# A decoder layer on one core: token-major x loaded and squared along the second column block, and a final scale folded into one product

## The chip, the core and the metric

The kernel runs on one core of a Trainium2 chip. It is judged by its device time in microseconds (us), the median of three runs: 1476.53 us (1476.25 to 1477.11). Inside the core, TensorE (PE) multiplies matrices into PSUM, VectorE (DVE) and ScalarE (ACT) do elementwise work, GpSimd (POOL) a little of it, and SyncE (SP) issues DMAs. Each engine takes its own list of instructions in order and waits on semaphores. ACT issues DMAs too, from the same list as its arithmetic.

## What is computed

One decoder layer over 256 tokens of width 2048, in float32. Cut to what matters here:

```python
h = rms_norm(x, norm_mix)
q, k, v, cx, cb, cc, ga, gc = split_in_proj(h @ w_in)     # 10240 columns
q = partial_rope(heads(q, 8), pos); k = partial_rope(heads(k, 8), pos)
...                                                       # attention, short convolution, gated merge
x = x + merged @ w_mix_out
...                                                       # cross-attention over 256 memory tokens
u = relu(rms_norm(x, norm_mlp) @ w_up)
x = x + (u * u) @ w_down
return rms_norm(x, norm_final)

def rms_norm(x, g):
    return x * rsqrt(mean(x * x, axis=-1) + 1e-6) * g
```

## The kernel before

Every weight is streamed from HBM once, in pieces of 256 rows by 512 columns (512 KB, `load_w`, issued by SP into six raw buffers). To keep float32 accuracy each piece is split (`split_w`, L61): ACT copies it rounded to the matmul type (`whi`, L66), DVE subtracts that from the raw piece (`wlo`, L67). The activations are split in the same way, and `tok_steps` (L97) makes three matmuls for each 128 rows and each half of the tokens: high times high, high times low, low times high. `tok_group` (L107) runs 16 such steps over a block of 512 columns, into two PSUM banks of the five that the matmuls share. Five pairs of split buffers stand between ACT and DVE on one side and PE on the other.

The norm of x is not applied ahead of the first projection. The feature-major copy of x (`xraw`, loaded from a transposed input) is multiplied by the gain and split (`split_scaled`, L133, into `hT`), and the factor of each token, `r1`, is multiplied in when a result leaves PSUM (`scaled`, L203, on ACT at L204). For `r1` the token-major x (`xtok`, four pieces of 512 KB) is loaded by ACT (L246), ACT squares it in eight pieces with a running sum (`sumsq`, L187, at L189), and `rstd` (L191) makes the factor on DVE and POOL. `xtok` is also the residual stream of everything that follows.

The column blocks at the start come in the order q, k, v (512 columns each), and again q, k, v. The first q block is written out by hand at L236 to L254: for each pair of steps x is scaled, the weights are split and matmuls run; the first four steps are single ones with loads of 128 and 256 KB, the rest pairs. The program gives the four x loads at the end of that block, and the squares behind them. In what order each engine takes its instructions is settled by a scheduler that reads the program and its dependences. A q or k block is rotated on DVE (`rotate`, L213) and transposed on PE (`qk_features`, L224).

At the end, the last 512 columns of the last projection are computed in three cuts: 512 columns for the first half of the tokens, then 256 and 256 for the second half (L494). Behind each cut `add_last` (L462) adds to the residual on DVE (L459), squares on ACT and multiplies by the final gain `gf` (L466); then the norm factor `rf` is made (L508 to L513), four pieces of 512 columns are multiplied by it (L514 to L519), and SP stores them (L520).

## Time and profile before

| | |
|---|---|
| median of three runs | 1476.53 us (1476.25 to 1477.11) |
| the profiled execution | 1476.77 us, span 1475.0 us |
| mean granted TensorE clock | 0.996 |
| PE, DVE, ACT busy | 1454.8, 820.9, 691.2 us |
| DMA | 281.27 MB, mean 191 GB/s |

The span runs from the first to the last instruction; the 1.8 us between it and the execution's time lie around it. A busy time adds up an engine's instructions. A row of a timeline has the start, the duration, the engine with the line of the program, what it writes and reads, and in brackets how long the engine stood idle and what released it. Tiles go by the names of the program's buffers: `S` stands for the large ones (`hT`, `xraw`, later ones), `raw`, `whi` and `wlo` for the weights, `tok` for `xtok`, `acc` for the PSUM banks of the matmuls, `junk` for what the squares write. Matmuls are pipelined and their ends modelled, so the distance from start to start tells their pace.

### The profile page before, as it was taken

The numbers are of one execution on the slowest core, as the hardware profiler recorded it, in microseconds if no ns is written. First come the engines' busy times: TensorE is split into PE (matmuls) and PEld (weight loads), VectorE is DVE, ScalarE is ACT, GpSimd is POOL, SyncE is SP. The second block draws the span as 40 slices with busy tenths as digits, with TensorE's granted clock in tenths as the row PEclk, the third lists the DMA queues.
The fourth block names the chain that finished last, engine by engine and source line by source line (L and its number), as shares of the span: only waits on it lengthen the run. The fifth ranks groups of instructions, "written<-read, shape, count | busy, mean of one in ns | idle before, by whom it ended". The sixth has DMA issues, their size and how long they took to land.

```text
span 1475.0 us, 18233 instructions
## 1 busy us (share of the span) xinstructions
PE 1454.8 (99%) x7064; PEld 1222.4 (83%) x7064; DVE 820.9 (56%) x976; ACT 691.2 (47%) x905; POOL 13.6 (1%) x21
## 2 busy tenths in 40 slices
PE   6999999999999999999999999999999999999997
PEld 5888888888888888888888888888888888888886
DVE  5545555765554646654476655556545555556554
ACT  6444544454444445554564443444434443445442
POOL 0000000000000000000000000000000000000011
PEclk9999999999999999999999999999999999999999
DMA  9666655576666667655555566565565556665652
GB/s 337 193 193 180 184 165 178 170 227 190 187 196 188 186 197 230 212 192 180 172 171 185 187 198 191 182 197 180 194 200 179 193 188 191 192 191 179 198 189 85
DMA packets 145158, 281.27 MB, mean 191 GB/s; under 512 B 8880, under 2 KB 9520, under 8 KB 144944
## 3 DMA queue, kind: packets, MB, share of 16 engines
q1 hardware_dynamic: 141888, 272.66, 58.9%
q10 hardware_dynamic: 3184, 7.45, 1.5%
q8 instruction: 55, 0.90, 0.2%
q14 instruction: 31, 0.25, 0.1%
HBM read 277.98 MB, written 2.10 MB: 190 GB/s over the span
## 4 chain that ended last, share of the span: by engine, by line
PE 98%; DMA 1%; ACT 1%; issue 0%; DVE 0%; POOLq 0%; POOL 0%; DVEq 0%; SPq 0%; ACTq 0%
PE acc L104 23%; PE acc L105 23%; PE acc L103 23%; PE acc L78 15%; PE acc L79 8%; PE aps L145 1%; PE acc L82 1%; DMA tok<-in_x_dram 1%; PE acc L81 1%; DMA raw<-in_w_in_dram 0%; ACT junk L189 0%; PE aps L315 0%; PE aps L270 0%; PE aps L438 0%; PE aps L407 0%
## 5 line engine op out<-in xcount | busy, mean ns | idle before, releaser
L67 DVE TENSOR_TENSOR wlo<-raw,whi 128x1024 fp32r<-128x1024 f32 (+1 forms) x510 | 618.7, 1222 | 561.2 <-ACT whi L66 547.5
L66 ACT ACTIVATE whi<-raw 128x1024 fp32r<-128x1024 f32 (+1 forms) x510 | 532.9, 1055 | 564.1 <-PE acc L105 386.2
L103 PE MATMUL acc<-whi,S 128*128 128x512 f32 x1512 | 584.9, 388 | 11.4 <-ACT whi L66 11.4
L105 PE MATMUL acc<-whi,S 128*128 128x512 f32 x1512 | 587.9, 389 | 0.0
L104 PE MATMUL acc<-wlo,S 128*128 128x512 f32 x1512 | 586.3, 388 | 0.3 <-DVE wlo L67 0.3
L103 PEld LDWEIGHTS acc<-whi,S 128*128 128x128 f32 x1512 | 284.6, 188 | 68.8 <-ACT whi L66 12.7
L78 PE MATMUL acc<-S,whi 128*128 128x512 f32 x960 | 341.6, 398 | 0.0
L104 PEld LDWEIGHTS acc<-wlo,S 128*128 128x128 f32 x1512 | 284.5, 188 | 58.8 <-DVE wlo L67 1.6
L105 PEld LDWEIGHTS acc<-whi,S 128*128 128x128 f32 x1512 | 284.7, 188 | 56.2
L79 PE MATMUL acc<-S,wlo 128*128 128x256 f32 x960 | 269.7, 281 | 0.0
L78 PEld LDWEIGHTS acc<-S,whi 128*128 128x128 f32 x960 | 180.4, 188 | 41.3
L79 PEld LDWEIGHTS acc<-S,wlo 128*128 128x128 f32 x960 | 181.3, 189 | 3.1
L474 ACT ACTIVATE blk<-acc 128x256 f32<-128x256 f32 x64 | 24.3, 380 | 36.0 <-PE acc L82 35.8
L189 ACT ACTIVATE junk<-tok 128x512 f32<-128x512 f32 (+1 forms) x33 | 20.2, 613 | 37.7 <-DVE tok L459 23.6
L459 DVE SCALAR_TENSOR_TENSOR tok<-acc,q,tok 128x512 f32<-128x512 f32 (+1 forms) x33 | 24.1, 731 | 18.0 <-PE acc L105 18.0
L130 ACT ACTIVATE S<-blk 128x512 fp32r<-128x512 f32 x32 | 20.0, 626 | 25.7 <-DVE blk L478 25.7
L475 DVE TENSOR_TENSOR blk<-acc,blk 128x256 f32<-128x256 f32 x64 | 27.0, 422 | 8.0 <-ACT blk L474 8.0
L131 DVE TENSOR_TENSOR S<-blk,S 128x512 fp32r<-128x512 f32 x32 | 22.1, 692 | 9.9 <-ACT S L130 8.4
L82 PE MATMUL acc<-S,whi 128*128 128x512 f32 x64 | 25.6, 400 | 0.0
L478 DVE SCALAR_TENSOR_TENSOR blk<-blk 128x512 f32<-128x512 f32 x32 | 22.0, 689 | 0.6
L204 ACT ACTIVATE blk<-acc,r 128x512 f32<-128x512 f32 x18 | 12.4, 689 | 15.5 <-PE acc L105 15.5
L81 PE MATMUL acc<-S,wlo 128*128 128x256 f32 x64 | 18.1, 283 | 0.0
(127 smaller groups left out, 466.2 us busy)
## 6 DMA issues: line engine op xcount, KB each, us to landing
raw<-in_w_in_dram SPq DMA_DIRECT2D x158, 512.0 KB, 4.2
raw<-in_w_up_dram SPq DMA_DIRECT2D x128, 512.0 KB, 4.0
raw<-in_w_down_dram SPq DMA_DIRECT2D x128, 512.0 KB, 4.3
raw<-in_w_mix_out_dram SPq DMA_DIRECT2D x32, 512.0 KB, 4.9
raw<-in_w_attn_out_dram SPq DMA_DIRECT2D x16, 512.0 KB, 4.3
raw<-in_w_conv_out_dram SPq DMA_DIRECT2D x16, 512.0 KB, 4.5
raw<-in_wkv_x_dram SPq DMA_DIRECT2D x16, 512.0 KB, 4.2
raw<-in_wq_x_dram SPq DMA_DIRECT2D x8, 512.0 KB, 3.9
```

The costliest lines, as they stand in the source:

```text
L66: nc.scalar.activation(hi[:, k:k + step, :], raw[:, k:k + step, :], AF.Copy)
L67: nc.vector.tensor_sub(lo[:, k:k + step, :], raw[:, k:k + step, :], hi[:, k:k + step, :].bitcast(F32))
L78: nc.tensor.matmul(ps, a, xs(k, 2), start=(k == 0), stop=False)
L79: nc.tensor.matmul(ps[:, S:], c, xs(k, 0), start=False, stop=False)
L81: nc.tensor.matmul(ps[:, S:], c, xs(k, 0), start=False, stop=False)
L82: nc.tensor.matmul(ps, a, xs(k, 2), start=(k == 0), stop=True)
L103: nc.tensor.matmul(ps, xh, wh, start=(k == 0), stop=False)
L104: nc.tensor.matmul(ps, xh, wl, start=False, stop=False)
L105: nc.tensor.matmul(ps, xl, wh, start=False, stop=(k == nk - 1))
L459: nc.vector.scalar_tensor_tensor(t, ps, q3[:, h:h + 1], t, op0=ALU.mult, op1=ALU.add)
L474: nc.scalar.activation(z[:, b, :], ps[:, S:], AF.Copy)
L475: nc.vector.tensor_add(z[:, b, :], ps[:, :S], z[:, b, :])
```

## The change

There are two edits. At the start, the first q block is taken out of the loop and runs without the x loads and squares. Its evacuation is put off: the next block (k) runs with a hook `norm1` that is called before each chunk of four steps; it issues one piece of x on ACT's queue and squares the piece before it, and both are bound to come behind the last weight split that ACT had been given by then (`issue_after`). The rope table's load moves there too. Behind the k block come the last two squares, the factor `r1`, and then the evacuations of the q and the k block.

At the end, the squares carry a factor so that their sum is the mean, the gain is no longer multiplied into the last cut of either half of the tokens but with the norm factor in one instruction, the stored pieces are cut at another place, and two of the four stores of each half are issued by ACT.

```diff
--- before.py
+++ after.py
@@ -58,12 +58,14 @@
             nc.sync.dma_start(raw[:, k:k + step, :], rows.rearrange("(k p) c -> p k c", p=P))
         return raw
 
+    last_split = [None]
+
     def split_w(raw, hi=None, lo=None, step=2):
         nk = raw.shape[1]
         hi = wsp.tile([P, nk, 512], F32R, name="whi") if hi is None else hi
         lo = wsp.tile([P, nk, 512], F32R, name="wlo") if lo is None else lo
         for k in range(0, nk, step):
-            nc.scalar.activation(hi[:, k:k + step, :], raw[:, k:k + step, :], AF.Copy)
+            last_split[0] = nc.scalar.activation(hi[:, k:k + step, :], raw[:, k:k + step, :], AF.Copy)
             nc.vector.tensor_sub(lo[:, k:k + step, :], raw[:, k:k + step, :], hi[:, k:k + step, :].bitcast(F32))
         return [(hi[:, k, :], lo[:, k, :]) for k in range(nk)]
 
@@ -104,9 +106,10 @@
             nc.tensor.matmul(ps, xh, wl, start=False, stop=False)
             nc.tensor.matmul(ps, xl, wh, start=False, stop=(k == nk - 1))
 
-    def tok_group(w, c0, kr0, nk, xs, evac):
+    def tok_group(w, c0, kr0, nk, xs, evac, along=lambda k0: None):
         ps = [psum_mm(), psum_mm()]
         for k0 in range(0, nk, 4):
+            along(k0)
             parts = weights(w, kr0 + k0, c0) + weights(w, kr0 + k0 + 2, c0)
             for h in range(2):
                 tok_steps(ps[h], h, k0, nk, parts, xs)
@@ -226,6 +229,27 @@
             nc.scalar.activation(qT[:, i, 4 * c + b:4 * c + b + 2, :], pt.rearrange("p (k s) -> p k s", k=2), AF.Copy)
         to_features(qk, 0, 4, ev)
 
+
+    ps0 = [psum_mm(), psum_mm()]
+    for q in range(8):
+        for k in range(2):
+            split_scaled(hT, 2 * q + k, xraw[:, 2 * q + k, :], g_of(0, 2 * q + k))
+        parts = split_w(first[q] or load_w(w_in, 2 * q, 2, 0), step=1 if q < 2 else 2)
+        for h in range(2):
+            tok_steps(ps0[h], h, 2 * q, KD, parts, hx)
+    r1sp = const.tile([P, 2, 4], F32, name="r1sp")
+
+    def norm1(k0):
+
+        with tc.issue_after(last_split[0].ins):
+            if k0 == 0:
+                nc.scalar.dma_start(csb, rope)
+            d = k0 // 4
+            nc.scalar.dma_start(xtok[:, :, d * 512:(d + 1) * 512], xv[:, :, d * 512:(d + 1) * 512])
+            if d:
+                for h in range(2):
+                    sumsq(r1sp[:, h, d - 1:d], xtok[:, h, (d - 1) * 512:d * 512], 512)
+
     for c in range(2):
         for i in range(2):
             qk = block()
@@ -234,24 +258,20 @@
                 scaled(qk[:, h, :], ps, r1, h)
                 rotate(qk, h)
             if i == c == 0:
-                ps = [psum_mm(), psum_mm()]
-                for q in range(8):
-                    for k in range(2):
-                        split_scaled(hT, 2 * q + k, xraw[:, 2 * q + k, :], g_of(0, 2 * q + k))
-                    parts = split_w(first[q] or load_w(w_in, 2 * q, 2, 0), step=1 if q < 2 else 2)
+                qk0, ev0 = qk, ev
+                continue
+            if c == 0:
+                ps1 = []
+                tok_group(w_in, i * AW + c * 512, 0, KD, hx, lambda h, ps: ps1.append(ps), norm1)
+                with tc.issue_after(last_split[0].ins):
                     for h in range(2):
-                        tok_steps(ps[h], h, 2 * q, KD, parts, hx)
-                    if q >= 4:
-                        o = (q - 4) * 512
-                        nc.scalar.dma_start(xtok[:, :, o:o + 512], xv[:, :, o:o + 512])
-                nc.scalar.dma_start(csb, rope)
-                sp = const.tile([P, 2, 4], F32, name="r1sp")
+                        sumsq(r1sp[:, h, 3:4], xtok[:, h, 1536:2048], 512)
+                r1 = rstd(r1sp, "r1")
                 for h in range(2):
-                    for d in range(4):
-                        sumsq(sp[:, h, d:d + 1], xtok[:, h, d * 512:(d + 1) * 512], 512)
-                r1 = rstd(sp, "r1")
+                    ev0(h, ps0[h])
+                qk_features(qk0, 0, 0)
                 for h in range(2):
-                    ev(h, ps[h])
+                    ev(h, ps1[h])
             else:
                 tok_group(w_in, i * AW + c * 512, 0, KD, hx, ev)
             qk_features(qk, i, c)
@@ -462,8 +482,10 @@
     def add_last(h, ps, o, n, i, engine):
 
         t = add_block(h, ps, o, n)
-        sumsq(ssf[:, h, i:i + 1], t, n)
-        engine.tensor_mul(t, t, gf[:, o:o + n])
+        junk = small("junk", (P, 512))
+        nc.scalar.activation(junk[:, :n], t, AF.Square, scale=D ** -0.5, accum_out=ssf[:, h, i:i + 1])
+        if engine:
+            engine.tensor_mul(t, t, gf[:, o:o + n])
 
     for g in range(NG):
         uT = big.tile([P, KG, 2, S], F32R, name="S2")
@@ -501,23 +523,28 @@
         parts += split_w(load_w(w_down, kr + 8 + k, 2, c0), wt[:, k:k + 2, 0, :], wt[:, k:k + 2, 1, :])
     for h, t, o, n in cuts:
         tok_steps(t[:, :n], h, 8, KG, parts, xu, o, n)
-        add_last(h, t[:, :n], c0 + o, n, 3 + o // 256, nc.vector)
         i = 3 + o // 256
-        if h == 1 and o == 0:
+        inner = h == 1 and o == 0
+        add_last(h, t[:, :n], c0 + o, n, i, nc.vector if inner else None)
+        if inner:
             continue
         pre = const.tile([P, 1], F32, name=f"pre{h}")
         nc.vector.reduce_sum(pre, ssf[:, h, :i], axis=AX.X)
-        nc.vector.tensor_scalar(pre, pre, 1.0 / D, EPS, op0=ALU.mult, op1=ALU.add)
+        nc.vector.tensor_scalar(pre, pre, EPS, None, op0=ALU.add)
         rf = const.tile([P, 1], F32, name=f"rf{h}")
-        nc.vector.tensor_scalar(rf, ssf[:, h, i:i + 1], 1.0 / D, pre, op0=ALU.mult, op1=ALU.add)
+        nc.vector.tensor_add(rf, ssf[:, h, i:i + 1], pre)
         nc.gpsimd.tensor_tensor(rf, rf, mhalf[:, :1], op=ALU.pow)
-        for c in range(4):
-            o = xtok[:, h, c * 512:(c + 1) * 512]
-            if c == 1:
-                nc.scalar.activation(o, o, AF.Copy, scale=rf)
+        e = c0 + o
+        for lo, hi, engine, queue in ((0, 512, nc.scalar, nc.sync), (512, 1024, nc.vector, nc.scalar),
+                                      (1024, e, nc.vector, nc.sync), (e, D, None, nc.scalar)):
+            y = xtok[:, h, lo:hi]
+            if engine is nc.scalar:
+                nc.scalar.activation(y, y, AF.Copy, scale=rf)
+            elif engine:
+                nc.vector.tensor_scalar(y, y, rf, None, op0=ALU.mult)
             else:
-                nc.vector.tensor_scalar(o, o, rf, None, op0=ALU.mult)
-            nc.sync.dma_start(ov[:, h, c * 512:(c + 1) * 512], o)
+                nc.vector.scalar_tensor_tensor(y, y, rf, gf[:, lo:hi], op0=ALU.mult, op1=ALU.mult)
+            queue.dma_start(ov[:, h, lo:hi], y)
 
 
 def _rope_table():
```

The scheduler makes of it the following. ACT at the start of the program, before: `L246` loads x, `L247` the rope table, `L134` scales x by the gain, `L66` splits a weight piece, `L189` squares a piece of x.

```order
L246 DMA tok<-in_x_dram 128x2x512 x2
L134 ACTIVATE S_84<-S_85,gcol 128x256 [waits DMAHW1_49,DMAHW0_49]
L66 ACTIVATE whi<-raw 128x512 [waits DMAHW2_49]
L246 DMA tok<-in_x_dram 128x2x512 x2
L247 DMA csb<-in_rope_dram 128x128 [waits DMAHW3_49]
L134 ACTIVATE S_84<-S_85,gcol 128x256 [waits DMAHW4_49]
L189 ACTIVATE junk,r1sp<-tok 128x512
L189 ACTIVATE junk,r1sp<-tok 128x512 [waits DMAHW5_49]
L66 ACTIVATE whi<-raw 128x512 [waits DMAHW6_49]
L189 ACTIVATE junk,r1sp<-tok 128x512 [waits DMAHW7_49,Activation_49]
L134 ACTIVATE S_84<-S_85,gcol 128x256 [waits DMAHW0_49]
L189 ACTIVATE junk,r1sp<-tok 128x512 [waits DMAHW1_49,Activation_49]
```

ACT at the same place, with the change (L137 is the scaling, L68 the split):

```order
L137 ACTIVATE S_84<-S_85,gcol 128x256 [waits DMAHW1_49,DMAHW0_49]
L68 ACTIVATE whi<-raw 128x512 [waits DMAHW2_49]
L137 ACTIVATE S_84<-S_85,gcol 128x256 [waits DMAHW3_49]
L68 ACTIVATE whi<-raw 128x512 [waits DMAHW4_49]
L137 ACTIVATE S_84<-S_85,gcol 128x256 [waits DMAHW5_49]
L68 ACTIVATE whi<-raw 128x512 [waits DMAHW6_49]
L137 ACTIVATE S_84<-S_85,gcol 128x256 [waits DMAHW7_49]
L68 ACTIVATE whi<-raw 128x512 [waits DMAHW0_49]
L137 ACTIVATE S_84<-S_85,gcol 128x256 [waits DMAHW1_49]
L137 ACTIVATE S_84<-S_85,gcol 128x256
L68 ACTIVATE whi<-raw 128x1024 [waits DMAHW2_49]
```

The loads and squares of x are gone from there, and scaling and split alternate. On ACT around the first evacuation, before (L204 evacuates, L226 copies the transposed result):

```order
L66 ACTIVATE whi<-raw 128x1024 [waits DMAHW3_49,DVE_49,PE_49]
L66 ACTIVATE whi<-raw 128x1024 [waits DMAHW4_49,DVE_49,PE_49]
L66 ACTIVATE whi<-raw 128x1024 [waits DMAHW5_49,DVE_49,PE_49]
L204 ACTIVATE blk<-acc,r_324 128x512 [waits PE_49,Pool_49]
L204 ACTIVATE blk<-acc,r_324 128x512 [waits PE_49]
L66 ACTIVATE whi<-raw 128x1024 [waits DMAHW6_49,DVE_49]
L66 ACTIVATE whi<-raw 128x1024 [waits DMAHW7_49,DVE_49,PE_49]
L66 ACTIVATE whi<-raw 128x1024 [waits DMAHW0_49,DVE_49,PE_49]
L226 ACTIVATE S_127<-aps 128x512 [waits PE_49] x2
```

ACT at the end of the second block, with the change, from the split of the k block's last pair on (L192 squares, L207 evacuates; the first two evacuations are the q block's, the third is the k block's first half):

```order
L68 ACTIVATE whi<-raw 128x1024 [waits DMAHW7_49,DVE_49,PE_49]
L192 ACTIVATE junk,r1sp<-tok 128x512 [waits DMAHW0_49,Activation_49]
L192 ACTIVATE junk,r1sp<-tok 128x512 [waits Activation_49]
L68 ACTIVATE whi<-raw 128x1024 [waits DMAHW1_49,DVE_49,PE_49]
L192 ACTIVATE junk,r1sp<-tok 128x512 [waits DMAHW3_49,Activation_49]
L192 ACTIVATE junk,r1sp<-tok 128x512 [waits Activation_49]
L68 ACTIVATE whi<-raw 128x1024 [waits DMAHW2_49,DVE_49,PE_49]
L68 ACTIVATE whi<-raw 128x1024 [waits DMAHW4_49,DVE_49,PE_49]
L207 ACTIVATE blk<-acc,r_471 128x512 [waits Pool_49]
L207 ACTIVATE blk<-acc,r_471 128x512
L207 ACTIVATE blk<-acc,r_471 128x512 [waits PE_49]
L68 ACTIVATE whi<-raw 128x1024 [waits DMAHW5_49,DVE_49,PE_49]
```

The last four squares and three splits of the v block stand ahead of the q block's evacuation, which waits for POOL's factor. DVE at the end of the program, before, behind the 256-column cut (L459 evacuates, L466 multiplies by the gain, L512 makes the factor's input, L519 multiplies by the factor):

```order
L466 TENSOR_TENSOR tok<-tok,S_5832 128x256 [waits Activation_49]
L509 TENSOR_REDUCE pre_11411<-ssf 128x1
L510 TENSOR_SCALAR pre_11411<-pre_11411 128x1 [waits DVE_49]
L459 SCALAR_TENSOR_TENSOR tok<-acc,q_5830,tok 128x256 [waits PE_49]
L466 TENSOR_TENSOR tok<-tok,S_5832 128x256 [waits Activation_49]
L512 TENSOR_SCALAR rf_11414<-ssf,pre_11411 128x1
L519 TENSOR_SCALAR tok<-tok,rf_11414 128x512 [waits Pool_49]
L519 TENSOR_SCALAR tok<-tok,rf_11414 128x512
L519 TENSOR_SCALAR tok<-tok,rf_11414 128x512 [waits DVE_49]
```

and with the change (L479, L488, L535, L544 are the same in turn, L546 multiplies by factor and gain):

```order
L488 TENSOR_TENSOR tok<-tok,S_5832 128x256 [waits Activation_49]
L532 TENSOR_REDUCE pre_11409<-ssf 128x1
L479 SCALAR_TENSOR_TENSOR tok<-acc,q_5830,tok 128x256 [waits PE_49]
L533 TENSOR_SCALAR pre_11409<-pre_11409 128x1 [waits DVE_49]
L535 TENSOR_TENSOR rf_11412<-ssf,pre_11409 128x1 [waits DVE_49,Activation_49]
L544 TENSOR_SCALAR tok<-tok,rf_11412 128x512 [waits Pool_49]
L544 TENSOR_SCALAR tok<-tok,rf_11412 128x768
L546 SCALAR_TENSOR_TENSOR tok<-tok,rf_11412,S_5832 128x256
```

One product by the gain is gone from the way to the factor, and the three products behind it have other widths.

## Rows read from the trace of the kernel before

**Rows 1.** The page: busy time of each engine

```profile
...
PE 1454.8 (99%) x7064; PEld 1222.4 (83%) x7064; DVE 820.9 (56%) x976; ACT 691.2 (47%) x905; POOL 13.6 (1%) x21
```

**Rows 2.** Waits of PE over the span: us in total, times, longest

```profile
...
PE acc L103 <- ACT whi L66: 11.4, 3, 5.9
```

**Rows 3.** Timeline of PE: start, us, what, idle before and releaser

```profile
...
5.88 1.22 PE L103 MATMUL acc<-whi,S 128*128 128x512 f32 x2 [5.88 <-ACT whi L66]
...
8.18 0.63 PE L105 MATMUL acc<-whi,S 128*128 128x512 f32 x1
10.99 0.73 PE L103 MATMUL acc<-whi,S 128*128 128x512 f32 x2 [2.18 <-ACT whi L66]
...
16.40 1.22 PE L103 MATMUL acc<-whi,S 128*128 128x512 f32 x2 [3.37 <-ACT whi L66]
...
18.70 0.63 PE L105 MATMUL acc<-whi,S 128*128 128x512 f32 x1
...
21.55 0.50 PE L104 MATMUL acc<-wlo,S 128*128 128x512 f32 x1 [0.26 <-DVE wlo L67]
...
34.42 0.39 PE L104 MATMUL acc<-wlo,S 128*128 128x512 f32 x1
34.64 0.39 PE L105 MATMUL acc<-whi,S 128*128 128x512 f32 x1
```

**Rows 4.** Chain that ended last, first 45 us: start, us, what

```profile
...
1.18 3.99 DMA raw<-in_w_in_dram
...
5.66 8.14 DMA tok<-in_x_dram
13.88 1.95 ACT junk L189 x6
```

**Rows 5.** Stretches of 1 us: busy time, PEclk, DMA share, GB/s

```profile
...
3.00:4.00 1.00, 0.00 (x0) 0.00 (x0) 0.00 (x0) 0.41 (x1) 0.00 (x0) 1.00 0.92 248
...
18.00:19.00 1.00, 1.00 (x4) 0.81 (x3) 0.81 (x3) 1.00 (x3) 0.48 (x1) 0.50 0.97 293
19.00:20.00 1.00, 1.00 (x5) 0.75 (x5) 1.00 (x3) 1.00 (x2) 0.78 (x1) 0.77 0.97 309
```

**Rows 6.** Two longer stretches, same columns

```profile
...
30.00:37.70 7.70, 7.70 (x36) 6.38 (x35) 6.12 (x7) 4.61 (x5) 0.00 (x0) 1.00 1.02 364
37.70:59.00 21.30, 21.30 (x100) 17.70 (x99) 10.42 (x17) 9.72 (x11) 0.00 (x0) 1.00 0.64 195
```

**Rows 7.** Timeline of ACT

```profile
...
3.60 0.51 ACT L134 ACTIVATE S<-S,gcol 128x256 fp32r<-128x256 f32 x1 [0.93 <-DMA gcol<-in_cols_dram]
5.19 0.63 ACT L66 ACTIVATE whi<-raw 128x512 fp32r<-128x512 f32 x1 [1.09 <-DMA raw<-in_w_in_dram]
...
37.79 0.69 ACT L204 ACTIVATE blk<-acc,r 128x512 f32<-128x512 f32 x1 [0.38 <-PE acc L105]
```

**Rows 8.** Groups of the first 40 us: busy us, mean ns, idle before

```profile
...
L67 DVE TENSOR_TENSOR wlo<-raw,whi 128x1024 fp32r<-128x1024 f32 x11 | 13.2, 1217 | 1.8 <-ACT whi L66 1.8
...
L135 DVE SCALAR_TENSOR_TENSOR S<-S,gcol,S 128x256 fp32r<-128x256 f32 x16 | 7.1, 478 | 6.9 <-ACT S L134 6.9
```

**Rows 9.** Tile tok, first 60 us: times from DMA issue to landing

```profile
...
DMA to landing us min/median/max: 5.8/7.5/8.1
```

**Rows 10.** Timeline of the last 9 us

```profile
...
1466.51 0.48 DVE L459 SCALAR_TENSOR_TENSOR tok<-acc,q,tok 128x256 f32<-128x256 f32 x1 [0.62 <-PE acc L105]
...
1467.62 0.42 DVE L466 TENSOR_TENSOR tok<-tok,S 128x256 f32<-128x256 f32 x1 [0.64 <-ACT junk L189]
1467.97 0.21 DVE L512 TENSOR_SCALAR rf<-ssf,pre 128x1 f32<-128x1 f32 x1
...
1468.84 0.72 ACT L517 ACTIVATE tok<-tok,rf 128x512 f32<-128x512 f32 x1 [1.25 <-POOL rf L513]
1468.84 1.28 DVE L519 TENSOR_SCALAR tok<-tok,rf 128x512 f32<-128x512 f32 x3 [0.67 <-POOL rf L513]
```

**Rows 11.** Two stretches of the end, columns as above

```profile
...
1470.00:1473.40 3.40, 0.00 (x0) 0.00 (x0) 0.12 (x1) 0.00 (x0) 0.00 (x0) 0.52 0.86 308
```

## The prediction

> **What bounds the kernel now.** I read the page's busy times first, then PE's waits, then the timeline at the two ends of the span. PE is busy for 1454.8 us of 1475.0 [rows 1], and over the whole span it waits in substance for one thing, the high halves of the weights at the start: three waits, 11.4 us together [rows 2]. Between 37.7 and 59 us it shows 21.30 us busy out of 21.30 [rows 6]. So nothing in the middle can be shortened by an edit that leaves the matmuls alone. What an edit can reach is the start, until PE runs without gaps, and the tail behind the last matmul.
>
> The start is read from PE's timeline [rows 3]. The first matmul is at 5.88 us, six run, PE waits 2.18 us, six run, PE waits 3.37 us to 16.40 us, and after a last wait of 0.26 us at 21.55 us the flow has no gap. The chain says why: it goes through the first weight load (landed 5.17 us), then through loads of token-major x from 5.66 to 13.80 us, then through squares on ACT [rows 4]. ACT takes its instructions in order; the squares of x stand between the splits that PE wants, and each waits for its piece of x. Beside that, the pieces of x share the DMA engines with the first weights.
>
> The account of the first column block in PE's time, to check the reading: waits 5.88 + 2.18 + 3.37 + 0.26 = 11.7 us. Its 96 matmuls at the pitch of the smooth part, 34.64 - 34.42 = 0.22 to 0.23 us (I use 0.227, [rows 3]), need 21.8 us. Three bursts ran slow: six matmuls took 8.81 - 5.88 = 2.93 us, 13.03 - 10.99 = 2.04 us and about 2.73 us from 16.40 us, where the smooth pitch gives 1.36 us, so 1.57 + 0.68 + 1.37 = 3.6 us more. Around the third burst the granted clock was 0.50 (the 1.2 GHz level) at 18 us and 0.77 on the way up at 19 us [rows 5], after PE had been waiting. The sum is 37.1 us; the block's second evacuation starts at 37.79 us [rows 7], so some 0.6 us of handovers stay unnamed.
>
> **The change, part by part.**
>
> *Start.* Four x loads of 512 KB, the small rope load and eight squares leave the first block and stand on ACT along the second. In the first block ACT then has only the scaling of x and the splits. I price each term as it will be.
>
> First matmul. The gains land at 3.60 us and the scaling of x takes 0.51 us [rows 7]; the first split took 5.88 - 5.19 = 0.69 us until PE started. With weights at hand the first matmul could therefore come at 3.60 + 0.51 + 0.69 = 4.8 us; with weights no earlier than before it stays at 5.88 us. The first weights are 256 KB behind 128 KB of x and 44 KB of gains on their way; at the 248 GB/s of 3 to 4 us [rows 5] these 428 KB take 1.7 us from about 2 us on, and the rest is landing. I take 5.0 us, near the early end, since the row shows the engines already full (share 0.92) with x loads among the bytes: gain 0.9 us (0 to 1.1).
>
> The waits of 2.18 and 3.37 us. Each of the first single steps needs 384 KB, 1.5 us at 248 GB/s, and PE works on one for 2.9 us at the low clock or 1.36 us at the high one. From step four on a pair of steps (768 KB) takes 2.1 us at 364 GB/s [rows 6] and costs DVE 2 x 0.48 + 1.22 = 2.2 us (two scalings and a split, [rows 8]), against 12 x 0.227 = 2.72 us on PE. So PE is the slowest of the three and both waits go, with the 0.26 us; I leave 0.3 us for single gaps: gain 5.5 us (3 to 5.8). That the queue of SP alone fills the engines is in the row of 30 to 37.7 us: x has long landed there and only weights move.
>
> The low clock. One cold burst stays, 1.57 us; the two others came after PE's waits and go with them: gain 0.68 + 1.37 = 2.0 us (0.5 to 2.0).
>
> Start together: 0.9 + 5.5 + 2.0 = 8.4 us, with bounds 3.5 and 8.9.
>
> *Second block.* Is the gain given back there? Added traffic: 2.1 MB over 96 x 0.227 = 21.8 us, 96 GB/s, on top of 195 GB/s [rows 6], so 291 GB/s where 364 were reached. The squares cost ACT the same as before, but now beside a PE that is five weight pairs behind the splits (five buffers), 13.6 us. Each piece of x has at least two chunks between its issue and its first square in ACT's order, and needs 5.8 to 8.1 us to land [rows 9]. The first block's two accumulators stay full until the norm factor is there. Five banks are shared, so the v block starts its first accumulator in the fifth, and its second matmul group, 12 matmuls later, is the first instruction that needs one back. The evacuations stand on ACT behind the third v split, whose buffer comes free when PE has four steps of the k block left (5.4 us). Split and two evacuations are at most 1.2 + 0.7 + 0.7 = 2.6 us (DVE's part of a split takes 1.22 us, [rows 8], an evacuation 0.69 us, [rows 7]), so they end some 3 us before the k block does, and nearly 6 us before PE asks. I cost this at nothing (0 to 1 us of loss, if the ACT queue drifts).
>
> *Tail.* The product with the gain before the last norm factor goes: the factor's input starts at 1467.97 us behind a product that began at 1467.62 us [rows 10], so the chain to the factor is up to 0.35 us shorter. Against that, the first piece to be stored was DVE's, a third of 1.28 us or 0.43 us behind the factor; now each queue's first store stands behind ACT's 0.72 us product, either by its data or because ACT itself issues it: 0.3 us later. The stores then run at 308 GB/s mean from 1470.0 to 1473.4 us [rows 11], 1 MB in about 3 us, which is transfer and not issue. DVE's last part is two plain products, 0.43 us for 512 columns and for 768 columns between that and its double (I take 0.6 us), and one with the gain, near the 0.48 us of the 256-column row [rows 10]: 1.5 us against 1.28 us, ahead of the end of the transfer in either case. Another risk: the two stores of the first half on ACT stand ahead of the square of the next piece, and a DVE product waits for that square ahead of the last evacuation. Together +0.1 to +0.5 us of gain on the one side and -0.5 us on the other; I take +0.2 us.
>
> On the second queue the Trainium skill ("DMA: Bandwidth & Descriptors", Issuing engines are not separate DMA queues) says that DMAs from several engines run on the same 16 engines and interleave, and that a second issuer saves issue time alone. By that rule the two-queue stores give nothing here, and x on ACT's queue in the second block is paid for with weight bandwidth, which is a rival below; the trace agrees as far as it shows the stores filling the engines from a single queue.
>
> *Sum.* 8.4 + 0.2 = 8.6 us, against the profiled execution's 1476.77 us: 1468.2 us. That execution is 0.24 us over the median of the runs, so against 1476.53 us the forecast is 1467.9 us.
>
> **Rivals.**
>
> *A starved start.* Without the x loads the singles still come at 248 GB/s or less, with 1 KB rows, and PE waits and falls to the low clock once more. For it: the rate of 3 to 4 us with full engines. Against: 364 GB/s later from the same queue. If the first block's 6.3 MB came at 248 GB/s throughout, they would be in at 2 + 25.4 = 27.4 us; with 1.5 us of split and 2.7 us of PE the block ends at 31.6 us in place of 37.7, less one more cold burst of 1.4 us: gain 4.7 us, 1471.8 us.
>
> *Only moved.* By the rule of the second queue above, the bytes of x still have to pass. As a mechanism here: if PE's supply in the second block were at its limit, 2.1 MB at 364 GB/s would push the weights back by 5.8 us, and 8.6 - 5.8 = 2.8 us stay: 1473.7 us, at the edge of no change. Against it: a DMA share of 0.64 in that stretch [rows 6].
>
> *Slower: the norm factor comes late.* Place: the last square on ACT waits for the last piece of x, the evacuation of the first accumulators waits for the factor, and PE needs a bank 12 matmuls into the v block. The squares also hold back the v splits behind them on ACT. Price: every microsecond beyond the cover is a microsecond of PE. It decides once the piece lands about 12 us later than I reckon, 20 us after its issue, and the kernel is slower only from another 8.6 us on; at 32 us it would be 1479.5 us. The row of 5.8 to 8.1 us under full engines [rows 9] speaks against it.
>
> **How the numbers follow.** The forecast 0.64, the starved start 0.21, only moved 0.09, slower 0.06. The forecast's own range is 1466.5 to 1469.5 us: down by the upper bounds of start and tail and the 0.6 us of handovers that may go too (10.0 us), up by a wait or two more in the singles (7 us). To hold 8 of 10 the range takes in most of the starved start: 1466.0 to 1471.9 us. A measurement of this kernel tells 0.2%, 2.95 us, from no change. The first two cases are faster by more than that, with a third of the third; most of the last is slower by more: faster 0.88, same 0.07, slower 0.05.
>
> **What would show it.** In the profile after: first matmul at 4.8 to 5.3 us; PE's waits behind it under 1 us together; one stretch of low granted clock at the start and none between 10 and 20 us; the first block's matmuls done by about 29 us; the four evacuations of the first two blocks near 46 to 52 us, with PE waiting for none of them; the last DVE products ending within half a microsecond of before in distance from the last matmul. A wait of PE for the splits between 8 and 20 us means the starved start; a wait behind the k block for ACT means the late factor; PE waits for weights between 30 and 55 us mean that the load was only moved.

## The result, and the profile after

The changed kernel takes 1469.26 us (median of four runs, 1468.71 to 1469.80) against 1476.82 us before in the same measurement (1476.25 to 1477.38): a ratio of 0.9949, 95% interval 0.9932 to 0.9966. That is 7.6 us less; the forecast was 1467.9 us. The profiled execution took 1469.29 us, 7.48 us under that of before, with a span of 1467.5 us.

Two marks split the gain. The last matmul starts at 1459.22 us, before at 1466.19 us (0.32 us ahead of the evacuation in [rows 10], as now): 6.97 us come from ahead of it. From there to the end of the span it is 8.28 us, before 8.81 us: 0.53 us come from the tail. I use these two marks, "last matmul" and "distance to the end", for every run below; spans are given to 0.1 us, so a distance to the end is good to about 0.05 us.

The page's busy times, which answer to [rows 1]:

```profile
...
PE 1453.2 (99%) x7064; PEld 1221.5 (83%) x7064; DVE 820.2 (56%) x974; ACT 692.1 (47%) x905; POOL 13.0 (1%) x21
...
```

The work is the same, to 1.6 us of PE. What changed is the waiting. PE's waits, as in [rows 2]:

```profile
...
PE acc L105 <- ACT whi L68: 5.7, 3, 4.9
PE acc L106 <- DVE wlo L69: 0.5, 1, 0.5
```

4.9 us of this are the first matmul; 1.38 us in three pieces are left of the 5.8 us behind it. Where they lie is in PE's timeline [rows 3]:

```profile
...
4.88 1.22 PE L105 MATMUL acc<-whi,S 128*128 128x512 f32 x2 [4.88 <-ACT whi L68]
...
7.61 0.71 PE L105 MATMUL acc<-whi,S 128*128 128x512 f32 x2
...
10.22 0.39 PE L107 MATMUL acc<-whi,S 128*128 128x512 f32 x1
10.87 0.73 PE L105 MATMUL acc<-whi,S 128*128 128x512 f32 x2 [0.25 <-ACT whi L68]
...
12.39 0.39 PE L107 MATMUL acc<-whi,S 128*128 128x512 f32 x1
13.38 0.73 PE L105 MATMUL acc<-whi,S 128*128 128x512 f32 x2 [0.60 <-ACT whi L68]
14.64 0.50 PE L106 MATMUL acc<-wlo,S 128*128 128x512 f32 x1 [0.53 <-DVE wlo L69]
...
15.21 0.40 PE L105 MATMUL acc<-whi,S 128*128 128x512 f32 x1
...
55.12 0.39 PE L105 MATMUL acc<-whi,S 128*128 128x512 f32 x1
...
```

The first six matmuls run at the low pitch (4.88 to 7.61 us, 2.73 us where the smooth pitch gives 1.36) and no matmul after them takes 0.43 us again; the first three behind a wait follow at 0.33 to 0.39 us. PE waits three times between 10.2 and 14.7 us. The last row shows the v block's matmul at 55.12 us that needs a bank back, with no wait ahead of it. The chain that ended last, answering to [rows 4], no longer goes through x or through squares:

```profile
...
4.96 7.28 DMA raw<-in_w_in_dram
12.27 1.07 ACT whi L68
13.36 1.24 DVE wlo L69
14.64 0.50 PE acc L106
...
```

It goes through the load of the first weight pair: issued at 4.96 us, landed at 12.27 us, split by ACT in 1.07 and by DVE in 1.24 us. Stretches of the same columns as [rows 5, 6]:

```profile
...
6.00:7.00 1.00, 1.00 (x4) 0.81 (x3) 0.25 (x1) 0.91 (x2) 0.00 (x0) 1.00 0.65 217
...
9.00:10.00 1.00, 1.00 (x7) 0.79 (x5) 0.40 (x1) 0.51 (x1) 0.00 (x0) 1.00 0.94 307
10.00:11.00 1.00, 0.75 (x4) 0.32 (x3) 0.24 (x2) 0.70 (x2) 0.00 (x0) 1.00 1.05 375
...
30.00:50.00 20.00, 20.00 (x90) 16.57 (x89) 10.09 (x15) 13.38 (x26) 0.71 (x1) 1.00 0.93 328
...
```

Between 5 and 10 us the DMA engines move 217 to 307 GB/s, from 10 us on 375 and more. In the second block they move 328 GB/s at a share of 0.93, where the share was 0.64. On ACT [rows 7] the first split now follows the first scaling at once, the last square ends at 44.6 us, and the evacuations come at 48 to 53 us:

```profile
...
3.65 0.51 ACT L137 ACTIVATE S<-S,gcol 128x256 fp32r<-128x256 f32 x1 [0.98 <-DMA gcol<-in_cols_dram]
4.20 0.63 ACT L68 ACTIVATE whi<-raw 128x512 fp32r<-128x512 f32 x1
...
44.11 0.62 ACT L192 ACTIVATE junk<-tok 128x512 f32<-128x512 f32 x1
...
48.12 1.25 ACT L207 ACTIVATE blk<-acc,r 128x512 f32<-128x512 f32 x2
49.88 0.69 ACT L207 ACTIVATE blk<-acc,r 128x512 f32<-128x512 f32 x1 [0.50 <-PE acc L107]
...
52.60 0.69 ACT L207 ACTIVATE blk<-acc,r 128x512 f32<-128x512 f32 x1 [0.30 <-PE acc L107]
...
```

The first two evacuations end at 49.37 us, 5.7 us before PE asks for the bank at 55.12 us. The end of the program, answering to [rows 10] (`L479` evacuates, `L535` makes the factor's input, `L542` and `L544` multiply by it, `L547` stores):

```profile
...
1459.22 0.28 PE L107 MATMUL acc<-S,S 128*128 128x256 f32 x1
1459.54 0.48 DVE L479 SCALAR_TENSOR_TENSOR tok<-acc,q,tok 128x256 f32<-128x256 f32 x1 [0.25 <-PE acc L107]
...
1460.66 0.16 DVE L535 TENSOR_TENSOR rf<-ssf,pre 128x1 f32<-128x1 f32 x1 [0.57 <-ACT junk L486]
...
1461.49 1.02 DVE L544 TENSOR_SCALAR tok<-tok,rf 128x512 f32<-128x512 f32 x2 [0.67 <-POOL rf L536]
1461.49 0.72 ACT L542 ACTIVATE tok<-tok,rf 128x512 f32<-128x512 f32 x1 [0.86 <-POOL rf L536]
1462.01 1.26 ACTq L547 DMA_DIRECT2D out_dram<-tok  x2
1462.23 0.83 SPq L547 DMA_DIRECT2D out_dram<-tok  x2
...
```

The factor's input comes 1.12 us behind the last evacuation's start, before 1467.97 - 1466.51 = 1.46 us. ACT issues its first store at 1462.01 us, while its own product (1461.49 + 0.72) still runs. That is 0.52 us behind the start of the products. The kernel before issued its first store, on SP, 0.51 us behind theirs (1468.84 us in [rows 10]):

```profile
...
1469.35 1.79 SPq L520 DMA_DIRECT2D out_dram<-tok  x4
```

### The profile page after: what moved, and what is told of

Its sections match the earlier page's. It is cut to its first block, busy times and chain, and to the rows that moved or that the text cites. A ratio compares the mean times of both kernels' runs of the same rounds, so it can differ in the third digit from the quotient of the medians.

```text
span 1467.5 us, 18231 instructions
## 1 busy us (share of the span) xinstructions
PE 1453.2 (99%) x7064; PEld 1221.5 (83%) x7064; DVE 820.2 (56%) x974; ACT 692.1 (47%) x905; POOL 13.0 (1%) x21
## 3 DMA queue, kind: packets, MB, share of 16 engines
q10 hardware_dynamic: 3760, 8.37, 1.7%
## 4 chain that ended last, share of the span: by engine, by line
PE 98%; DMA 0%; issue 0%; SPq 0%; DVE 0%; ACT 0%; POOLq 0%; POOL 0%; DVEq 0%; ACTq 0%
PE acc L106 24%; PE acc L105 24%; PE acc L107 24%; PE acc L80 15%; PE acc L81 8%; PE aps L148 1%; PE acc L84 1%; PE acc L83 1%; DMA raw<-in_w_in_dram 0%; PE aps L335 0%; PE aps L290 0%; PE aps L427 0%; PE aps L458 0%; PE aps L308 0%; PE aps L304 0%
## 5 line engine op out<-in xcount | busy, mean ns | idle before, releaser
L68 ACT ACTIVATE whi<-raw 128x1024 fp32r<-128x1024 f32 (+1 forms) x510 | 533.1, 1055 | 558.3 <-PE acc L107 377.5
L479 DVE SCALAR_TENSOR_TENSOR tok<-acc,q,tok 128x512 f32<-128x512 f32 (+1 forms) x33 | 24.1, 731 | 17.0 <-PE acc L107 17.0
L134 DVE TENSOR_TENSOR S<-blk,S 128x512 fp32r<-128x512 f32 x32 | 22.1, 692 | 9.9 <-ACT S L133 8.4
L192 ACT ACTIVATE junk<-tok 128x512 f32<-128x512 f32 x24 | 15.0, 625 | 12.7 <-DVE tok L375 11.5
L207 ACT ACTIVATE blk<-acc,r 128x512 f32<-128x512 f32 x18 | 12.3, 687 | 13.4 <-PE acc L107 13.4
```

The lines of the kernel that those rows point to most:

```text
L68: last_split[0] = nc.scalar.activation(hi[:, k:k + step, :], raw[:, k:k + step, :], AF.Copy)
L479: nc.vector.scalar_tensor_tensor(t, ps, q3[:, h:h + 1], t, op0=ALU.mult, op1=ALU.add)
```

## The experiments

The question was where the 7 us of the start come from, why they are not the 8.4 us of the forecast, and which half of the tail's edit pays. "Supply" stands for the theories by which the first weights land late (beside the bytes of x, or cut into too small transfers), "order" for the squares standing in ACT's way, "width" for the pair-wide splits of the first steps that keep PE waiting.

| kernel | median us (range) | ratio to before [95%] | last matmul | distance to the end |
|---|---|---|---|---|
| changed kernel | 1469.26 (1468.71-1469.80) | 0.9949 [0.9932, 0.9966] | 1459.22 | 8.28 |
| start_only | 1469.80 (1469.62-1471.72) | 0.9957 [0.9942, 0.9972] | 1461.07 | 8.83 |
| tail_only | 1475.97 (1475.66-1476.79) | 0.9997 [0.9988, 1.0007] | 1466.29 | 8.21 |
| loads_early | 1473.34 (1473.08-1473.84) | 0.9978 [0.9969, 0.9988] | 1463.30 | 8.3 |
| squares_early | 1470.80 (1470.51-1470.99) | 0.9960 [0.9946, 0.9975] | 1460.68 | 8.2 |
| both_early | 1473.47 (1473.31-1474.21) | 0.9979 [0.9969, 0.9988] | 1464.17 | 8.2 |
| split_single | 1468.46 (1468.30-1468.89) | 0.9945 [0.9931, 0.9960] | 1458.82 | 8.3 |
| load_single | 1468.08 (1467.41-1468.98) | 0.9943 [0.9928, 0.9958] | 1458.40 | 8.2 |
| pairs_from_2 | 1469.43 (1468.67-1471.01) | 0.9953 [0.9937, 0.9970] | 1459.63 | 8.1 |
| warm_pe | 1468.30 (1467.26-1468.79) | 0.9940 [0.9927, 0.9954] | 1458.82 | 8.2 |
| late_factor | 1469.53 (one run) | | 1459.51 | 8.2 |
| fold_only | 1469.55 (one run) | | 1459.33 | 8.37 |
| queues_only | 1470.05 (one run) | | 1459.55 | 8.75 |

**The two halves apart: start_only and tail_only.** The first has the changed start with the old `add_last` and last loop, the second the old start with the new ones.

> Only the start of the change; the end is that of the kernel before. By my account (PE's last matmul starts 6.97 us earlier in the changed kernel, the rest of the gain lies behind it) the last matmul starts 7.0 us earlier than before and the distance from it to the end of the span is that of before, 8.8 us: 7.0 us faster than before. If the two edits help each other, or the end gives more than 0.5 us, it is under 6.5 us.

> Only the end of the change; the start is that of the kernel before. Expected: the last matmul where it was before (start at 1466.2 us), the distance from its start to the end of the span 8.3 us in place of 8.8 us, 0.5 us in all, which is less than three rounds can tell; the trace decides. My prediction had 0.2 us here.

The start alone is worth 1476.42 - 1469.80 = 6.6 us, the tail alone 0.45 us by the medians and 0.6 us by its distance to the end; its ratio alone could not tell it from nothing. The sum, 7.1 us, is the gain of the whole to within the runs' spread. The profiled execution of start_only is the slowest of its four, its last matmul 1.85 us behind the changed kernel's. One of its stretches shows why:

```profile
...
16.00:17.00 1.00, 1.00 (x4) 0.78 (x3) 1.00 (x2) 0.82 (x2) 0.00 (x0) 0.50 1.07 393
...
```

Behind waits like those of the changed kernel (0.96 us to 13.59 and 0.53 us to 14.85 us) the granted clock fell to 0.50, the 1.2 GHz level, for some 3 us. The other three runs lie within 0.33 us of each other.

**What of the start is the loads, what the squares: loads_early, squares_early, both_early.** All have the changed kernel's second block and tail. loads_early issues x where the old kernel did, two pieces at once and two behind the first split:

```diff
+    for d in range(2):
+        load_x(d)
...
+            if q == k == 0:
...
+                    for d in range(2, 4):
+                        load_x(d)
...
-            nc.scalar.dma_start(xtok[:, :, d * 512:(d + 1) * 512], xv[:, :, d * 512:(d + 1) * 512])
```

squares_early leaves the loads late and puts eight more squares on ACT at the old places, ahead of the scalings (the first list) and behind them (the second), of a weight piece that is there anyway; both_early has both edits:

```diff
+            act(lambda: nc.scalar.activation(junk, first[0][:, 0, :], AF.Square, accum_out=extra[:, c:c + 1]))
...
+                squares((0, 0, 1, 0)[n] if n < 4 else 0)
...
+                squares((0, 2, 3, 2)[n] if n < 4 else 0)
```

> The changed kernel with its four loads of token-major x issued at the start as in the kernel before (two ahead of the first scaling, two behind the first split, on ACT), while the squares stay along the second block. Supply theory (the x loads take the first weights' share of the DMA engines): most of the 7.0 us is lost again, first matmul at about 5.9 us, PE waits of 3 us and more before 20 us, 4 to 6 us slower than the changed kernel. Order theory (the squares stand in ACT's list ahead of the splits): at most 1.5 us slower, the later first matmul.

> The changed kernel with eight more squares of 128x512 on ACT between the second scaling and the fourth split, where the kernel before has its squares; they read the first weight piece, which has landed, and their sums are not used. The loads of x stay along the second block. Order theory: 8 x 0.8 us = 6.4 us more on ACT in the first steps, of which ACT's idle time there (2.8 us) takes a part: 3.5 to 5 us slower than the changed kernel, with a second cold burst. Supply theory: 0 to 1.5 us slower, since the weights that ACT waits for come no later.

> The changed kernel with the two earlier edits together: the four loads of token-major x at the start, as before, and eight extra squares on ACT between the second scaling and the fourth split, at the places the squares of x had, but of the first weight piece, which has landed; the squares of x stay along the second block. Alone the loads cost 4.1 us of the start's 7.0 and the squares 1.5; 1.4 us are left. If the two add, the last matmul starts 5.5 us later than in the changed kernel, at 1464.8 us, and the time is 1474.8 us (1474.3 to 1475.3): the rest is then that the squares of before waited for their pieces of x. If the rest is that both together open a further low-clock burst, squares that wait for nothing cost it too: last matmul at 1466.2 us, 1476.2 us.

Against the changed kernel the loads cost 4.1 us (1473.34 - 1469.26), the squares 1.5 us, both together 4.2 us: neither figure expected of the two together. The old start with the new tail (tail_only) is at 1475.97 us, 2.5 us more. What it has and both_early has not is that the squares wait for their pieces of x. ACT's timeline of the kernel before has that wait in three rows:

```profile
...
9.69 0.63 ACT L189 ACTIVATE junk<-tok 128x512 f32<-128x512 f32 x1 [0.66 <-DMA tok<-in_x_dram]
...
12.19 0.63 ACT L189 ACTIVATE junk<-tok 128x512 f32<-128x512 f32 x1 [1.26 <-DMA tok<-in_x_dram]
...
13.88 0.63 ACT L189 ACTIVATE junk<-tok 128x512 f32<-128x512 f32 x1 [0.57 <-DMA tok<-in_x_dram]
...
```

0.66 + 1.26 + 0.57 = 2.49 us, in front of the splits that PE wants, and of the size that is missing. So of the start's 6.7 us by these medians 4.1 go with the bytes of x beside the first weights. The squares' own time adds 0.1 on top, less than the 0.3 us by which the kernel before itself differs between the two measurements (1476.42 and 1476.72 us). It hides while ACT waits for weights and for the transposed x anyway: in the first 22 us these waits are 8.0 us in loads_early and 3.4 us in both_early. The 2.5 us that are left go with the squares' waiting for x; this is by difference and by the three rows, and no run puts that wait back alone. Between the profiled executions of both_early and tail_only the last matmul differs by 2.1 us: PE waits 1.5 us longer in tail_only (10.2 against 8.7 us), and the rest is slower matmuls, so the 2.5 us hold some of the low clock as well. In both_early PE waits in all nearly as long as with the loads alone (8.0 and 0.5 us):

```profile
...
PE acc L105 <- ACT whi L269: 8.2, 3, 6.8
PE acc L106 <- DVE wlo L270: 0.5, 1, 0.5
```

**Why 7.0 us and not 8.4: split_single, load_single, pairs_from_2.** In the changed kernel the first four steps load and split single pieces of 128 rows, the others pairs. load_single goes on with singles up to the eighth step:

```diff
-        step = 1 if q < 2 else 2
+        step = 1 if q < 4 else 2
...
-        parts = split_w(first[q] or load_w(w_in, 2 * q, 2, 0), step=1 if q < 2 else 2)
+        parts = split_w(first[q] or load_w(w_in, 2 * q, 2, 0), step=1 if q < 4 else 2)
```

split_single has the second of these edits alone; pairs_from_2 has `q < 1` in both places, singles for two steps only.

> The changed kernel with the splits of steps 4 to 7 in single steps (128x512 in place of 128x1024); all loads as they are. In the changed kernel PE waits 0.60 us for ACT's split of the first pair and 0.53 us for DVE's, behind a pair of weights that landed at 12.27 us. Width theory (the pair's two splits are too long a way from landing to matmul): ACT's part is 0.43 us shorter and DVE's 0.53 us, so both waits go or nearly and the last matmul comes about 1 us earlier. Supply theory (the pair simply lands late): at most 0.5 us.

> The changed kernel with loads and splits of steps 4 to 7 in single steps, 128 KB of x and 256 KB of weights each. Width theory: step 4 needs half the bytes of the pair, so its weights land 1 us earlier and the waits between 10 and 15 us go: 1 to 1.5 us faster than the changed kernel. Supply theory (too little is in flight: eight transfers at a time, and the small ones ran at 217 to 307 GB/s): more small transfers keep the rate low for longer, PE waits 2 us or more between 8 and 20 us, 1 to 2 us slower.

> The changed kernel with loads and splits of steps 2 and 3 as a pair as well (single steps 0 and 1 alone). Supply theory: fewer and larger transfers, the rate between 4 and 10 us rises from about 260 to over 300 GB/s, the pair 4 and 5 lands 1 us earlier and the wait there goes; step 2 comes later by its pair (landing, ACT and DVE 1 us): 0 to 1 us faster. Width theory: 1 to 2 us slower, since PE waits once more, at about 9 us, for a pair's splits.

With single splits one wait of 0.31 us is left; with single loads as well there is none behind the first matmul. PE's waits in load_single:

```profile
...
PE acc L105 <- ACT whi L68: 5.1, 1, 5.1
```

and PE's timeline of the same kernel:

```profile
...
5.08 1.22 PE L105 MATMUL acc<-whi,S 128*128 128x512 f32 x2 [5.08 <-ACT whi L68]
...
7.81 1.05 PE L105 MATMUL acc<-whi,S 128*128 128x512 f32 x2
...
10.34 0.63 PE L105 MATMUL acc<-whi,S 128*128 128x512 f32 x2
...
```

Its DMA engines moved no more between 4 and 14 us, 307 GB/s on the mean against 314, so it isn't the rate that went up. What went is the wait for a whole pair: ACT splits step 4 at 10.47 us here, where the changed kernel's pair is there at 12.27 us. But twelve matmuls ran at the low pitch here (5.08 to 10.34 us, 5.26 us where 12 x 0.227 = 2.72 are due), so PE also asked later. The last matmul came 0.82 us earlier than in the changed kernel. pairs_from_2, with about as many slow matmuls, has waits of 0.68 and 0.53 us and its last matmul 1.23 us behind load_single's; its time is level with the changed kernel's, which neither expectation had (its rate between 4 and 10 us is 277 GB/s against 261). The medians put load_single 1.2 us under the changed kernel, with intervals that overlap; so the waits are seen to go in the traces, but the gain in time is not clear of noise.

**The first matmuls at the low clock: warm_pe.** load_single with two plain float32 products of a tile of ones ahead:

```diff
+    for _ in range(2):
+        nc.tensor.matmul(heat, ones[:, 0:P], ones, start=True, stop=True)
```

> The kernel with single loads and splits up to step 7, with two matmuls of 128x512 plain float32 on a tile of ones ahead of the first real one; their result is not used. In the changed kernel PE stands idle until 4.88 us and its first six matmuls (and in other runs the next six) take 0.43 us in place of 0.227 us. If that low clock is only the answer to the idle time ahead, work on PE from about 1.3 us on moves the rise to the high clock ahead by some 3 us: the first real steps run at 1.36 us, 1.2 to 2.5 us earlier in the last matmul if the weights keep up; if they do not, waits of the splits come back between 6 and 12 us and half of that is lost. Against 1468.1 us: 1465.8 to 1467.5 us. If the idle time is not the cause, no change or, with the two matmuls in the way, up to 0.5 us slower.

The forecast missed. PE's timeline:

```profile
...
1.49 3.78 PE L159 MATMUL aps<-ones 128*128 128x512 f32 x4 [1.49 <-DVE ones L156]
4.87 1.25 PE L105 MATMUL acc<-whi,S 128*128 128x512 f32 x2
...
7.60 0.63 PE L105 MATMUL acc<-whi,S 128*128 128x512 f32 x2
...
18.40 0.73 PE L105 MATMUL acc<-whi,S 128*128 128x512 f32 x2 [0.89 <-ACT whi L68]
...
```

PE is busy from 1.49 us, and still the first six real matmuls run at the low pitch, with the change at 7.60 us, as in the changed kernel (7.61 us). This gives load_single with only six slow matmuls, and shows what an earlier clock buys there. PE gets to the first pair of weights sooner and waits 0.89 us for its high half, and at 19.66 us 0.53 us more for its low half. ACT's timeline says for what:

```profile
...
17.29 1.06 ACT L68 ACTIVATE whi<-raw 128x1024 fp32r<-128x1024 f32 x1 [2.03 <-DMA raw<-in_w_in_dram]
...
```

The pair lands at 17.29 us, ACT had stood idle 2.03 us for it. In load_single the pair was there at 16.86 us and PE, slower, asked for it at 18.54 us. The last matmul is at 1458.82 us, 0.4 us behind load_single's and 0.4 us ahead of the changed kernel's, which had the same first matmul and the same pitch. So with narrow pieces the arrival of the weights is the next limit, and the slow first matmuls cost little as long as it is.

**How far the slower rival was: late_factor.** The last piece of x is loaded behind the k block's last split instead of one chunk earlier.

```diff
+            if d < 3:
+                nc.scalar.dma_start(xtok[:, :, d * 512:(d + 1) * 512], xv[:, :, d * 512:(d + 1) * 512])
...
+                    nc.scalar.dma_start(xtok[:, :, 1536:], xv[:, :, 1536:])
```

> The changed kernel with the fourth piece of x issued behind the last split of the second block, some 8 us later, so that squares, norm factor and the four evacuations come about that much later. In the changed kernel the last evacuation of the first block ends at 49.4 us and PE asks for its bank at 55.1 us, a cover of 5.7 us. The scheduler puts the second half of the v block's first chunk 12 matmuls later here, which adds 2.7 us of cover: together about what the piece is late, so PE waits 0 to 1 us there and the last matmul is within 1 us of the changed kernel. If the cover were smaller than I think (the slower case of my prediction), PE waits 2 us and more near 55 us.

ACT's timeline shows the four evacuations:

```profile
...
52.49 2.40 ACT L207 ACTIVATE blk<-acc,r 128x512 f32<-128x512 f32 x4
...
```

The first evacuation is 4.4 us later than in the changed kernel and nothing is lost: PE has no wait behind 15 us, and the one run lies within the changed kernel's range. Two evacuations take some 1.2 us, so the first block's banks are free at about 53.7 us, still 1.4 us ahead of the 55.12 us at which the changed kernel asks for one. This run itself asks later, by the other order of its v block that the expectation names, so it does not test the changed kernel's cover of 5.7 us to its end.

**The tail's two edits: fold_only and queues_only.** One keeps the new products and gives all stores to SP; the other keeps the old products and gives two of four stores to ACT. fold_only:

```diff
-        for lo, hi, engine, queue in ((0, 512, nc.scalar, nc.sync), (512, 1024, nc.vector, nc.scalar),
-                                      (1024, e, nc.vector, nc.sync), (e, D, None, nc.scalar)):
+        for lo, hi, engine, queue in ((0, 512, nc.scalar, nc.sync), (512, 1024, nc.vector, nc.sync),
+                                      (1024, e, nc.vector, nc.sync), (e, D, None, nc.sync)):
```

queues_only, against start_only:

```diff
-        for c in range(4):
+        for c in (1, 0, 2, 3):
...
-            nc.sync.dma_start(ov[:, h, c * 512:(c + 1) * 512], o)
+            queue = nc.scalar if c in (0, 3) else nc.sync
+            queue.dma_start(ov[:, h, c * 512:(c + 1) * 512], o)
```

> The changed kernel with all stores at the end on SP again; the gain stays folded into the last product. The factor comes 0.35 us earlier as in the changed kernel, but the first store waits for ACT's product of 0.72 us. If the end is set by when the first store starts (transfer bound), the distance from the start of the last matmul to the end of the span is 8.6 us (before 8.8, changed 8.3). If the two queues give nothing, as my prediction took it, it is 8.3 us as in the changed kernel.

> The changed kernel's start with the end of the kernel before, and only its stores shared between the queues: ACT's own product and one of DVE's are stored by SP, two of DVE's by ACT. If the end is set by when the first store starts, the first one starts as before (DVE's product, 0.43 us behind the factor) and the distance from the last matmul to the end of the span is 8.7 us; if issue time on SP set the end, 8.3 us or less.

The end of fold_only in time:

```profile
...
1459.33 0.28 PE L107 MATMUL acc<-S,S 128*128 128x256 f32 x1
...
1461.59 0.72 ACT L542 ACTIVATE tok<-tok,rf 128x512 f32<-128x512 f32 x1 [0.86 <-POOL rf L536]
...
1462.11 1.79 SPq L547 DMA_DIRECT2D out_dram<-tok  x4
...
```

and that of queues_only:

```profile
...
1459.55 0.28 PE L107 MATMUL acc<-S,S 128*128 128x256 f32 x1
...
1462.20 0.72 ACT L537 ACTIVATE tok<-tok,rf 128x512 f32<-128x512 f32 x1 [1.25 <-POOL rf L533]
...
1462.72 1.13 ACTq L541 DMA_DIRECT2D out_dram<-tok  x2
...
```

With one queue the distance to the end is 8.37 us, with two and the old products 8.75, with both edits 8.28, with neither 8.83 (start_only). By these the fold is worth 0.46 to 0.47 us and the second queue about 0.1 us, which is no more than the rounding of two spans and less than the spread of the distance among the kernels with the changed tail (8.1 to 8.3 us). In each of the two the first store is issued 0.52 us behind the products' start, when DVE's first product is done and ACT's is not; so no first store waited for ACT's product, and the case of 8.6 us for fold_only did not arise. The Trainium skill ("DMA: Bandwidth & Descriptors", Issuing engines are not separate DMA queues) says that a second issuer saves issue time alone; these two pairs of distances agree.

## Why the prediction was right, point by point

**Bound and direction: right.** PE's matmuls bound the kernel and its waits at the start were the thing to win. The three runs with loads and squares put back show it, and the forecast's mechanism (squares waiting for x, x sharing the engines with the first weights) is both of its large parts: the bytes of x by a run of their own (loads_early), the squares' waiting by difference.

**First matmul: right.** 4.88 us, foreseen 5.0: a gain of 1.0 us for 0.9. The gains still land first (3.65 us), and the scaling, the split and the first matmul follow without a gap. The mark moves between executions: with the old start it is at 5.49 us in tail_only, with the changed one at 4.91 us in start_only and 5.06 us in fold_only and queues_only.

**The waits: the term that was mis-sized most.** The prediction put it as "PE is the slowest of the three and both waits go, with the 0.26 us; I leave 0.3 us for single gaps". Measured are 1.38 us of named waits. Around them PE loses 1.11 us that carry no name: from 10.22 to 15.21 us eleven matmuls take 4.99 us, where 11 x 0.227 = 2.50 us are due, and 1.38 of the 2.49 us too many are in brackets. The step compared paces (2.1 us of load and 2.2 us of DVE against 2.72 us of PE for a pair). A pace holds once buffers are full. At the first pair nothing is ahead of PE, and what counts is the delay: both halves must have landed (12.27 us), then come 1.07 us on ACT and 1.24 us on DVE before PE has all of it. Halving these pieces (load_single) left the rate of the loads as it was and took every wait behind the first matmul away; net the traces put it at 0.4 us (warm_pe against the changed kernel, with the same pitch), 1.2 us (load_single against pairs_from_2) and 1.2 us by the medians, of the 1.4 us that the start fell short. The rest lies in when the weights land, as warm_pe's wait for the first pair shows; how much of it is not settled.

**The low clock: one burst fewer, where the gain was reckoned with two.** The third burst of the kernel before (from 16.40 us, 1.37 us over the smooth pitch) has no counterpart in the changed kernel, and the first is the same in both: 2.30 us from its first matmul to its sixth. The second burst, entered at 0.68 us, is misread. Its five distances from 10.99 us to the row below are 1.52 us, and those from 10.87 to 12.39 us in the changed kernel, behind a wait of 0.25 us, are 1.52 us too:

```profile
...
12.51 0.51 PE L105 MATMUL acc<-whi,S 128*128 128x512 f32 x1
```

So this slowness came back behind the waits that are left, and is part of the 1.11 us above. (In tail_only, with the same old start, these six matmuls did take 0.43 us each; the bursts differ between executions.) That the first burst holds up to twelve matmuls in some kernels, and that one can come back behind the waits that are left (start_only), was not foreseen.

**The sum of the start.** The second block's first matmul starts 6.95 us earlier, so nearly all of the 6.97 us lies in the first block; before and after:

```profile
...
37.59 0.39 PE L103 MATMUL acc<-whi,S 128*128 128x512 f32 x1
```

```profile
...
30.64 0.61 PE L105 MATMUL acc<-whi,S 128*128 128x512 f32 x2
```

The first matmul gave 1.0 us, the named waits 5.81 - 1.38 = 4.43 us, and what is left, 1.52 us, is slow matmuls and gaps around waits. The forecast had 0.9, 5.5 and 2.0: the waits fell 1.1 us short and the low clock 0.5 us, the first matmul gave 0.1 us more, and so 7.0 came of 8.4.

**Second block: right.** No wait behind 15 us, four evacuations at 48.1 to 53.3 us (foreseen 46 to 52), a cover of 5.7 us (nearly 6). late_factor came 4.4 us later for nothing lost. The rate, 328 GB/s, was higher than the 291 reckoned, and still below the 364 GB/s of [rows 6] and the 375 to 408 GB/s of 10 to 15 us. "Only moved" and the slower rival are out. (The slower rival's last figure is off by its own terms: level at 28.6 us, it comes to 1479.9 us at 32 us and not 1479.5; nothing hung on it.)

**The starved start: a part of it came.** Its mark appeared, waits between 8 and 20 us, and up to 10 us the rate was near its 248 GB/s. It did not hold the whole block (375 GB/s and more from 10 us on), so the waits fell 1.1 us short of the forecast, and not the 3.7 us by which this rival was under it. Two signs named for the forecast failed with it: the waits behind the first matmul are 1.38 us and not under 1 us, and the first block's matmuls end at 30.6 us and not by about 29.

**Tail: right in direction, wrong in one term.** +0.2 us was foreseen (0.5 at most), 0.53 measured. The factor came 0.34 us earlier (foreseen up to 0.35). The step that failed is "each queue's first store stands behind ACT's 0.72 us product, either by its data or because ACT itself issues it: 0.3 us later". ACT issued the store 0.52 us behind the start of its product, 0.20 us before that product ended, as soon as DVE's piece was done; before, the first store stood 0.51 us behind. So the 0.3 us were never lost.

## What to carry to other kernels

Where a pipeline starts, reckon the delay of the first piece through every stage (landing, then each engine's part), and not only the pace of each; smaller first pieces can take waits away without any more bandwidth, and a faster clock pays only up to the next arrival. Work that only some later step needs, loads and what waits for them alike, belongs behind the first stretch, as long as the chain from it to its user has a cover that can be read in the trace. At the end of a program an instruction taken off the serial way to a factor counts in full; a second queue for transfers that already fill the engines counts for almost nothing.

## What the runs showed of the hardware

- A DMA that ACT issues does not wait for the ACT instruction ahead of it to end: issue at 1462.01 us, product from 1461.49 to 1462.21 us.
- The rise of PE's clock at the start moves from execution to execution. Four kernels have the same start; in their profiles six (changed kernel, fold_only), seven (queues_only) and nine (start_only) of the first matmuls are slow, and twelve in load_single and split_single. In the granted-clock column the first burst does not show (1.00 throughout); only the pitch does, 0.43 us against 0.23. The Trainium skill ("TensorE: Matmul & The Clock Gate", What's actually happening) calls the number of cold matmuls run-variable; the traces agree, with 6 to 12.
- Two plain float32 products from 1.49 to 5.27 us ahead did not bring it below the six of the changed kernel (warm_pe). Whether another kind of work would stays open.
- With several transfers of 128 to 512 KB in flight at the start, the weight pair issued at 4.96 us took 7.28 us to land, at 217 to 307 GB/s on the engines between 5 and 10 us.
